# One reciprocal and one product with the gates per head, in place of one of each per query block

## The chip, the cores and the metric

The kernel runs on one core of a Trainium2 chip, in one launch. The metric is the device time of an execution in microseconds, as a median over runs. A core has five engines that work side by side, each through its own instruction queue in order: PE (matrix products; PEld is its weight load), DVE (VectorE), ACT (ScalarE), POOL (GpSimd) and SP, which here only issues transfers.

## The reference, cut to what matters

A two-layer decoder trunk over 512 tokens of width 1024. Each layer is a gated feed-forward half-step, a mixer, and a second gated feed-forward half-step. The mixer merges a pooling branch with an attention branch of 16 heads of width 64, and each head adds three attentions, each weighted by a gate:

```
out = gc[..., 0:1] * o_cmp + gc[..., 1:2] * o_slc + gc[..., 2:3] * o_win
# o_slc, o_win: p = masked_softmax(s, mask);  o = p @ v
# masked_softmax: exp(s - max) / sum(exp(s - max))
```

With 512 tokens there are 8 blocks of 64 keys and 16 would be selected, so the selected branch sees all earlier keys, and so does the window of 512. The two branches therefore need the same kind of causal softmax, each over its own keys; `gates` holds the sigmoids of the gates, three for each head and token.

## The kernel before

All products run in float32 split in a high and a low part, three matmuls in place of one (`mm3`, lines 121 to 123). The weights are streamed from memory, and ACT and DVE split each piece (lines 114 and 115). The feed-forward steps are long rows of such projection matmuls, each with 512 columns.

In the mixer, `head_probs` and `head_out` handle one head each. `head_probs(h)` goes over four query blocks of 128 tokens. For each block and each of two branches (selected, window) PE makes the scores (lines 645 and 655), DVE adds the distance term and finds the row minimum (line 634, `softmax_num`), and ACT takes the exponential and its row sum (line 636). The row sums of a head lie in one tile `c` of 128 x 8, a column for each pair of block and branch. Then, for each query block, DVE inverts two columns of `c` (line 660), multiplies them with two gates (line 661), and scales the two blocks of exponentials by them (line 664). `head_out(h)` transposes the scaled blocks on PE (line 677) into three banks for each branch; the first bank takes key block 0 of all four query blocks. ACT and DVE split each bank into `ph` and `pl` (lines 114 and 115), and PE multiplies these with the values (line 691).

The program is written as a list of steps: `head_probs(h)`, then `head_out(h-1)`, then one or two units of projection work that fill the time (the lists `gp`, `ga` and `q`). The order in which instructions stand on each engine is not the written order: a scheduler orders them when the program is built, by which of them are ready, and it mixes the projection matmuls of the fill between the matmuls of the heads. PE and DVE both run 16 heads in each of two layers in this way; these two stretches are called head stages below.

Of the kernel before, what the change touches and what calls it, by code (L numbers as in the profile page):

```python
# [14 lines left out]
ALU = mybir.AluOpType  # L15
# [4 lines left out]
TB = T // P  # L20
# [31 lines left out]
class Trunk:  # L52
# [566 lines left out]
    def head_probs(self, h):  # L619

        nc = self.nc
        g, q = h // 8, self.qs.pop(h)
        m, c = self.sm(8, "m"), self.sm(8, "c")
        probs = self.probs[h] = {}

        def slot():
            i = self.tpos % 16
            self.tpos += 1  # L630
            return self.tbuf[i // 8][:, i % 8]

        def softmax_num(t, sp, i, nk):
            nc.vector.tensor_tensor_reduce(t, sp, self.dist[:, T - nk :], SLOPES[h], 3e38,  # L634
                                           ALU.add, ALU.min, m[:, i : i + 1])
            nc.scalar.activation(t, t, AF.Exp, scale=-1.0, bias=m[:, i : i + 1],  # L636
                                 accum_out=c[:, i : i + 1])

        for qb in range(TB):
            nk = P * (qb + 1)  # L640
            qq = q[:, qb * P : qb * P + P]
            if qb < 2:
                sp = self.bank("sc")[:, : 2 * nk]
                for i, K in enumerate((self.KH[g], self.KL[g])):
                    nc.tensor.matmul(sp, qq, K[:, :, :nk], start=i == 0, stop=i == 1)  # L645
                t2 = slot()[:, : 2 * nk].rearrange("p (r k) -> p r k", r=2)
                s2 = sp.rearrange("p (r k) -> p r k", r=2)
                for br in range(2):
                    softmax_num(t2[:, br], s2[:, br], 2 * qb + br, nk)
                    probs[qb, br] = t2[:, br]  # L650
            else:
                for br in range(2):
                    sp = self.bank("sc")[:, :nk]
                    for i, K in enumerate((self.KH[g], self.KL[g])):
                        nc.tensor.matmul(sp, qq, K[:, br, :nk], start=i == 0, stop=i == 1)  # L655
                    t = slot()[:, :nk]
                    softmax_num(t, sp, 2 * qb + br, nk)
                    probs[qb, br] = t
            ci = c[:, 2 * qb : 2 * qb + 2]
            nc.vector.reciprocal(ci, ci)  # L660
            nc.vector.tensor_mul(ci, ci, self.gates[:, qb, 3 * h + 1 : 3 * h + 3])
            for br in range(2):
                t = probs[qb, br]
                nc.vector.tensor_scalar(t, t, ci[:, br : br + 1], None, ALU.mult)

    def head_out(self, h):
        nc = self.nc
# [247 lines left out]
```

## Time and profile before

| | |
|---|---|
| median of 3 runs | 2397.09 us (2396.93 to 2399.38) |
| the profiled execution | 2397.52 us, span in the trace 2395.7 us |
| PE busy in the span | 2363.0 us, 99% |
| DVE busy in the span | 1398.9 us, 58% |
| ACT busy in the span | 977.4 us, 41% |
| head stage of the first layer | 497.2 to 757.4 us |
| head stage of the second layer | 1676.0 to 1936.3 us |

Busy shares are means over stages. The digits of DVE in 40 slices run from 3 and 4 in the feed-forward stages to 9 in the head stages, while PE shows 9 in all but the first and the last. The records of matmuls overlap, since they are pipelined. Records on DVE overlap a little too: an instruction's record runs on while the next has begun.

### The profile page before, as it was taken

The page shows a single profiled execution, that of the slowest core. Times are in us where ns is not written, and L with a number is a line of the kernel's source. Part 1 is how long each engine was busy: PE and PEld are TensorE (multiplying, and loading weights), DVE is VectorE, ACT ScalarE, POOL GpSimd, SP SyncE. Part 2 cuts the span into 40 slices and gives each one's busy share as a digit, 9 for nine tenths or more (in the row PEclk, how much of TensorE's full clock was granted, in tenths as well). Part 3 has the DMA queues.
Part 4 walks back from the last instruction along what each step waited for, and adds up shares of the span by engine and source line. Part 5 has one row for each costly group of instructions (what it writes and reads, how often), then busy time and mean ns, then how long its engine had stood idle before and what let it go on. Part 6 is the DMA issues. An engine that isn't in the chain of part 4 may idle for free.

```text
span 2395.7 us, 28552 instructions
## 1 busy us (share of the span) xinstructions
PE 2363.0 (99%) x11042; PEld 1955.6 (82%) x11042; DVE 1398.9 (58%) x2684; ACT 977.4 (41%) x1689; POOL 51.5 (2%) x106
## 2 busy tenths in 40 slices
PE   8999999999999999999999999999999999999998
PEld 6888888778888888888888888887888887888887
DVE  4434346768988544443544443567988975434444
ACT  4222235556666432222332222345666664322222
POOL 1000000000001000000000000000000010000000
PEclk9999999999999999999999999999999999999999
DMA  5323224522124432323223232334222253232321
GB/s 159 104 90 105 89 97 140 158 82 62 58 76 153 138 105 89 101 93 101 92 89 105 89 105 90 119 115 156 71 71 80 71 185 110 88 106 88 106 79 62
DMA packets 226007, 244.24 MB, mean 102 GB/s; under 512 B 8688, under 2 KB 206416, under 8 KB 225872
## 3 DMA queue, kind: packets, MB, share of 16 engines
q1 hardware_dynamic: 225696, 242.37, 31.6%
q8 instruction: 87, 1.43, 0.3%
q14 instruction: 48, 0.39, 0.1%
q10 hardware_dynamic: 176, 0.05, 0.0%
HBM read 223.53 MB, written 18.87 MB: 101 GB/s over the span
## 4 chain that ended last, share of the span: by engine, by line
PE 58%; issue 15%; DVE 1%; POOL 1%; ACT 0%; DMA 0%; POOLq 0%; DVEq 0%; ACTq 0%; SPq 0%
PE ps_mm L122 9%; PE ps_mm L121 9%; PE ps_mm L123 9%; PE ps_pv L691 4%; PE ps_sc L121 3%; PE ps_sc L123 3%; PE ps_sc L122 3%; PE ps_pt L121 3%; PE ps_pt L122 3%; PE ps_pt L123 3%; PE ps_pt L677 3%; PE ps_sc L655 2%; PE ps_sc L645 1%; PE ps_sc L584 0%; DMA bP<-dB 0%
## 5 line engine op out<-in xcount | busy, mean ns | idle before, releaser
L114 ACT ACTIVATE wh<-wr 128x1024 fp32r<-128x1024 f32 (+1 forms) x392 | 408.8, 1043 | 1082.5 <-PE ps_mm L122 399.8
L115 DVE TENSOR_TENSOR wl<-wr,wh 128x1024 fp32r<-128x1024 f32 (+1 forms) x392 | 470.1, 1200 | 78.8 <-ACT wh L114 77.3
L121 PE MATMUL ps_sc<-xh,wh 128*128 128x512 f32 x704 | 276.8, 393 | 2.2 <-ACT x L840 2.2
L123 PE MATMUL ps_sc<-xh,wl 128*128 128x512 f32 x704 | 274.7, 390 | 0.0
L122 PE MATMUL ps_sc<-xl,wh 128*128 128x512 f32 x704 | 274.4, 390 | 0.0
L122 PE MATMUL ps_mm<-act,wh 128*128 128x512 f32 x704 | 274.4, 390 | 0.0
L123 PE MATMUL ps_mm<-act,wl 128*128 128x512 f32 x704 | 273.9, 389 | 0.0
L121 PE MATMUL ps_pt<-xh,wh 128*128 128x512 f32 x704 | 273.9, 389 | 0.0
L122 PE MATMUL ps_pt<-xl,wh 128*128 128x512 f32 x704 | 273.9, 389 | 0.0
L123 PE MATMUL ps_pt<-xh,wl 128*128 128x512 f32 x704 | 273.9, 389 | 0.0
L121 PE MATMUL ps_mm<-act,wh 128*128 128x512 f32 x704 | 273.3, 389 | 0.0
L342 DVE SCALAR_TENSOR_TENSOR x<-ps_mm,x 128x512 f32<-128x512 f32 x96 | 66.4, 692 | 239.7 <-PE ps_mm L123 239.7
L333 DVE TENSOR_TENSOR u<-ps_pt,R 128x512 f32<-128x512 f32 x88 | 60.9, 692 | 245.6 <-PE ps_pt L123 245.6
L121 PE MATMUL ps_mm<-xh,wh 128*128 128x512 f32 x512 | 203.2, 397 | 0.0
L325 DVE TENSOR_TENSOR z<-ps_sc,R 128x512 f32<-128x512 f32 x88 | 60.9, 692 | 242.7 <-PE ps_sc L123 242.6
L123 PE MATMUL ps_mm<-xh,wl 128*128 128x512 f32 x512 | 200.8, 392 | 0.0
L122 PE MATMUL ps_mm<-xl,wh 128*128 128x512 f32 x512 | 200.6, 392 | 0.0
L121 PEld LDWEIGHTS ps_sc<-xh,wh 128*128 128x128 f32 x704 | 132.6, 188 | 30.9 <-ACT x L840 2.6
L636 ACT ACTIVATE tbuf<-tbuf,m 128x128 f32<-128x128 f32 (+3 forms) x256 | 142.2, 556 | 36.2 <-DVE m L634 28.3
L122 PEld LDWEIGHTS ps_sc<-xl,wh 128*128 128x128 f32 x704 | 132.6, 188 | 28.1 <-issue 1.0
L122 PEld LDWEIGHTS ps_mm<-act,wh 128*128 128x128 f32 x704 | 132.2, 188 | 28.5 <-DVE act L115 1.3
L123 PEld LDWEIGHTS ps_sc<-xh,wl 128*128 128x128 f32 x704 | 132.5, 188 | 27.9
(238 smaller groups left out, 3870.7 us busy)
## 6 DMA issues: line engine op xcount, KB each, us to landing
wr<-in_ffn_w_gate_dram SPq DMA_DIRECT2D x44, 1024.0 KB, 5.3
wr<-in_ffn_w_up_dram SPq DMA_DIRECT2D x44, 1024.0 KB, 5.3
wr<-in_w_in_dram SPq DMA_DIRECT2D x34, 1024.0 KB, 5.2
wr<-in_ffn_w_down_dram SPq DMA_DIRECT2D x32, 1024.0 KB, 4.9
wr<-in_ffn_w_down_dram SPq DMA_DIRECT2D x16, 768.0 KB, 4.2
wr<-in_w_branch_nsa_dram SPq DMA_DIRECT2D x8, 1024.0 KB, 5.3
wr<-in_w_out_dram SPq DMA_DIRECT2D x8, 1024.0 KB, 5.3
dx<-x SPq DMA_DIRECT2D x16, 256.0 KB, 2.8
```

The source lines that it names most:

```text
L114: self.nc.scalar.activation(hi, src, AF.Copy)
L115: self.nc.vector.tensor_sub(lo, src, f32(hi))
L121: self.nc.tensor.matmul(out, lh, rh, start=first and i == 0, stop=False)
L122: self.nc.tensor.matmul(out, lh, rl, start=False, stop=False)
L123: self.nc.tensor.matmul(out, ll, rh, start=False, stop=last and i == n - 1)
L325: nc.vector.tensor_mul(z, g, self.R)
L333: nc.vector.tensor_mul(u, up, self.R)
L342: nc.vector.scalar_tensor_tensor(x, o, 0.5, x, ALU.mult, ALU.add)
L636: nc.scalar.activation(t, t, AF.Exp, scale=-1.0, bias=m[:, i : i + 1], accum_out=c[:, i : i + 1])
L655: nc.tensor.matmul(sp, qq, K[:, br, :nk], start=i == 0, stop=i == 1)
L677: nc.tensor.transpose(tp[:, w : w + P], probs[qb, br][:, kb * P : kb * P + P], self.ident)
L691: nc.tensor.matmul(out[:, T - n :], lhsT, rhs, start=i == 0, stop=i == len(ops) - 1)
```

## The change

The reciprocal and the product with the gates move out of the loop over the query blocks. They now run once for a head, over all eight columns of `c`, when all eight row sums are there; after that a second loop scales all eight blocks. All line numbers from 664 on grow by one: the reciprocal stands on line 659, the product on 661, the scaling on 665, the transposes on 678, the products with the values on 692.

```
-            ci = c[:, 2 * qb : 2 * qb + 2]
-            nc.vector.reciprocal(ci, ci)
-            nc.vector.tensor_mul(ci, ci, self.gates[:, qb, 3 * h + 1 : 3 * h + 3])
+        nc.vector.reciprocal(c, c)
+        c3 = c.rearrange("p (b r) -> p b r", r=2)
+        nc.vector.tensor_mul(c3, c3, self.gates[:, :, 3 * h + 1 : 3 * h + 3])
+        for qb in range(TB):
             for br in range(2):
-                t = probs[qb, br]
-                nc.vector.tensor_scalar(t, t, ci[:, br : br + 1], None, ALU.mult)
+                t, i = probs[qb, br], 2 * qb + br
+                nc.vector.tensor_scalar(t, t, c[:, i : i + 1], None, ALU.mult)
```

The scheduler orders the head stages anew. On PE the matmuls before the first head stage, between the two, and nearly all after the second stand in the same order as before.

**First place: DVE, at the end of the first head of a layer.** The rows run from the score pass (line 634, here over 512 keys) of the last query block to the scaling of that block; `qn` and `q` are a query projection, `pc` the compressed branch, `wl` a split of weights. Before:

```order
L634 ISA tbuf,m<-ps_sc,dist 128x512
L634 ISA m 128x1
L661 TENSOR_TENSOR c<-c,gates 128x2
L568 SCALAR_TENSOR_TENSOR qn<-ps_mm,small,R 128x512
L664 TENSOR_SCALAR tbuf<-tbuf,c 128x384 x2
L660 RECIPROCAL c<-c 128x2
L634 ISA tbuf,m<-ps_sc,dist 128x128
L634 ISA m 128x1
L661 TENSOR_TENSOR c<-c,gates 128x2
L573 TENSOR_TENSOR q<-qn,q 64x512
L664 TENSOR_SCALAR tbuf<-tbuf,c 128x512 x2
```

The same place after the change:

```order
L115 TENSOR_TENSOR wl<-wr,wh 128x1024
L616 TENSOR_TENSOR pc<-ps_pt,pc 64x512
L659 RECIPROCAL c<-c 128x8
L568 SCALAR_TENSOR_TENSOR qn<-ps_mm,small,R 128x512
L661 TENSOR_TENSOR c<-c,gates 128x8
L634 ISA tbuf,m<-ps_sc,dist 128x128
L634 ISA m 128x1
L665 TENSOR_SCALAR tbuf<-tbuf,c 128x128 x2
L665 TENSOR_SCALAR tbuf<-tbuf,c 128x256 x2
L665 TENSOR_SCALAR tbuf<-tbuf,c 128x384 x2
L665 TENSOR_SCALAR tbuf<-tbuf,c 128x512 x2
L573 TENSOR_TENSOR q<-qn,q 64x512 x2
```

The eight scalings of a head now stand in one run behind the one product with the gates; the split `wl` has come ahead of them, one `q` has gone behind them.

**Second place: PE, the first head's transposes.** `ps_mm_3813` (before) and `ps_mm_3801` (after) are the same projection of the fill, whose matmuls with `xh_2371`, `xl_2372` are its seventh to ninth; `ps_pt_3738` and `ps_pt_3726` are the bank of key block 0, whose fourth transpose reads the last query block. Before:

```order
L121 MATMUL ps_mm_3813<-xh_2371,wh_3649 128x512
L122 MATMUL ps_mm_3813<-xl_2372,wh_3649 128x512
L123 MATMUL ps_mm_3813<-xh_2371,wl_3650 128x512
L677 MATMUL ps_pt_3738<-ident_64,tbuf_3518 128x128
L677 MATMUL ps_pt_3747<-ident_64,tbuf_3518 128x128
L677 MATMUL ps_pt_3755<-ident_64,tbuf_3518 128x128 x2
```

After:

```order
L121 MATMUL ps_mm_3801<-xh_2371,wh_3643 128x512
L122 MATMUL ps_mm_3801<-xl_2372,wh_3643 128x512
L678 MATMUL ps_pt_3726<-ident_64,tbuf_3518 128x128
L678 MATMUL ps_pt_3735<-ident_64,tbuf_3518 128x128
L678 MATMUL ps_pt_3743<-ident_64,tbuf_3518 128x128
L123 MATMUL ps_mm_3801<-xh_2371,wl_3644 128x512
L678 MATMUL ps_pt_3726<-ident_64,tbuf_3518 128x128
L678 MATMUL ps_pt_3735<-ident_64,tbuf_3518 128x128
L678 MATMUL ps_pt_3743<-ident_64,tbuf_3518 128x128 x2
```

The transposes of the earlier query blocks stand later, between the projection matmuls; the fourth one still follows the ninth matmul of this projection.

**Third place: PE, the transposes of the fourteenth head.** `ps_pt_6082` (before) and `ps_pt_5992` (after) are its bank of key block 0, and `ps_pv_5975` and `ps_pv_5891` gather the head before it. Before:

```order
L691 MATMUL ps_pv_5975<-ph_5955,V_2733 128x512
L691 MATMUL ps_pv_5975<-pl_5956,V_2733 128x512
L691 MATMUL ps_pv_5975<-ph_5963,V_2733 128x384
L677 MATMUL ps_pt_6082<-ident_64,tbuf_3519 128x128 x2
L677 MATMUL ps_pt_6082<-ident_64,tbuf_3518 128x128 x2
```

After:

```order
L692 MATMUL ps_pv_5891<-pc_5640,Vc_3441 128x512
L655 MATMUL ps_sc_5972<-KH_2647,q_5298 128x512
L655 MATMUL ps_sc_5972<-KL_2649,q_5298 128x512
L655 MATMUL ps_sc_5977<-KH_2647,q_5298 128x512
L655 MATMUL ps_sc_5977<-KL_2649,q_5298 128x512
L678 MATMUL ps_pt_5992<-ident_64,tbuf_3519 128x128 x2
L678 MATMUL ps_pt_5992<-ident_64,tbuf_3518 128x128 x2
```

The bank now follows the last product of the head before it, and the last two score pairs (`ps_sc_5972`, `ps_sc_5977`) of the head after it.

## Rows read from the trace of the kernel before

**Rows 1.** The page: span, busy time, share and instructions of two engines.
```profile
span 2395.7 us, 28552 instructions
...
PE 2363.0 (99%) x11042; PEld 1955.6 (82%) x11042; DVE 1398.9 (58%) x2684; ACT 977.4 (41%) x1689; POOL 51.5 (2%) x106
```

**Rows 2.** Stretches: length, PE, PEld, DVE, ACT, POOL busy, granted clock, DMA share, GB/s.
```profile
480.00:490.00 10.00, 8.06 (x26) 6.78 (x26) 3.29 (x10) 3.63 (x9) 0.00 (x0) 0.60 0.14 51
490.00:500.00 10.00, 10.00 (x44) 8.08 (x43) 1.89 (x3) 2.14 (x3) 0.00 (x0) 0.89 0.19 64
497.20:757.40 260.20, 258.53 (x1389) 214.51 (x1387) 235.24 (x727) 176.17 (x438) 6.45 (x7) 1.00 0.25 79
1676.00:1936.30 260.30, 258.48 (x1389) 214.42 (x1387) 235.37 (x727) 176.14 (x438) 5.50 (x5) 1.00 0.25 80
```

**Rows 3.** Single lines on DVE: count, shortest, median, longest in ns.
```profile
L660 DVE RECIPROCAL c<-c x128: 145/160/168, 505.8 to 1921.8; 128x2 f32<-128x2 f32 x128
...
L661 DVE TENSOR_TENSOR c<-c,gates x128: 140/156/524, 506.4 to 1922.4; 128x2 f32<-128x2 f32 x128
...
L664 DVE TENSOR_SCALAR tbuf<-tbuf,c x256: 269/380/488, 507.4 to 1923.3; 128x128 f32<-128x128 f32 x32, 128x256 f32<-128x256 f32 x32, 128x384 f32<-128x384 f32 x32, 128x512 f32<-128x512 f32 x32
...
L604 DVE RECIPROCAL cc<-cc x8: 246/248/252, 505.0 to 1878.5; 128x16 f32<-128x16 f32 x8
...
L606 DVE TENSOR_TENSOR cc<-cc,gates x8: 173/176/178, 505.4 to 1878.9; 128x16 f32<-128x16 f32 x8
```

**Rows 4.** Waits of PE's matmuls: us in total, times, longest.
```profile
PE ps_pt L610 <- POOL ec L607: 2.0, 8, 0.3
```

**Rows 5.** Timeline of DVE in the first head: start, us, engine, line.
```profile
507.41 0.47 DVE L664 TENSOR_SCALAR tbuf<-tbuf,c 128x128 f32<-128x128 f32 x2
507.80 0.15 DVE L660 RECIPROCAL c<-c 128x2 f32<-128x2 f32 x1
507.88 0.53 DVE L634 CUSTOM_DVE_ANT_0 tbuf<-ps_sc,dist 128x384 f32<-128x384 f32 x1
...
510.69 0.61 DVE L664 TENSOR_SCALAR tbuf<-tbuf,c 128x256 f32<-128x256 f32 x2
...
512.03 0.15 DVE L661 TENSOR_TENSOR c<-c,gates 128x2 f32<-128x2 f32 x1
512.11 0.75 DVE L568 SCALAR_TENSOR_TENSOR qn<-ps_mm,small,R 128x512 f32<-128x512 f32 x1
512.78 0.74 DVE L664 TENSOR_SCALAR tbuf<-tbuf,c 128x384 f32<-128x384 f32 x2
...
513.89 0.69 DVE L573 TENSOR_TENSOR q<-qn,q 64x512 fp32r<-64x512 f32 x1
514.61 0.88 DVE L664 TENSOR_SCALAR tbuf<-tbuf,c 128x512 f32<-128x512 f32 x2
```

**Rows 6.** Timeline of PE there: the group with the fourth transpose.
```profile
515.12 0.39 PE L123 MATMUL ps_mm<-xh,wl 128*128 128x512 f32 x1
515.35 0.60 PE L677 MATMUL ps_pt<-ident,tbuf 128*128 128x128 f32 x4
```

**Rows 7.** Timeline of DVE: the last scalings of the thirteenth and fourteenth head.
```profile
708.04 0.88 DVE L664 TENSOR_SCALAR tbuf<-tbuf,c 128x512 f32<-128x512 f32 x2
...
720.71 0.88 DVE L664 TENSOR_SCALAR tbuf<-tbuf,c 128x512 f32<-128x512 f32 x2
```

**Rows 8.** Timeline of PE: the transposes that follow those two.
```profile
711.21 0.60 PE L677 MATMUL ps_pt<-ident,tbuf 128*128 128x128 f32 x4
...
721.48 0.60 PE L677 MATMUL ps_pt<-ident,tbuf 128*128 128x128 f32 x4
```

**Rows 9.** The page's groups: split of weights, exponentials; busy us, mean ns of one.
```profile
L115 DVE TENSOR_TENSOR wl<-wr,wh 128x1024 fp32r<-128x1024 f32 (+1 forms) x392 | 470.1, 1200 | 78.8 <-ACT wh L114 77.3
...
L636 ACT ACTIVATE tbuf<-tbuf,m 128x128 f32<-128x128 f32 (+3 forms) x256 | 142.2, 556 | 36.2 <-DVE m L634 28.3
```

**Rows 10.** Timeline of PE: the wait ahead of the clock's fall.
```profile
482.09 0.39 PE L121 MATMUL ps_pv<-w2h,hh 128*128 128x64 f32 x1 [1.94 <-issue]
```

## The prediction

> **What bounds the kernel now.** I read the busy shares of the page first. PE is busy for 2363.0 of 2395.7 us, 99%; DVE, on which every changed instruction runs, for 1398.9 us, 58% [rows 1]. A mean over stages can hide a stage in which DVE sets the pace, so the second view is the busy time of the two head stages alone, the only places where lines 660 to 664 run [rows 2]. There DVE is busy for 235 of 260 us, 90%, but PE for 258.53 of 260.20 and 258.48 of 260.30, at the full granted clock (1.00). PE is thus idle for 1.67 and 1.82 us, 3.49 us together, and nothing done on DVE in these stages can win more than that by ending waits, as long as PE keeps its matmuls. It does: the scheduler deals out the same matmuls, in another order. The third view is what PE's matmuls waited for [rows 4]: 2.0 of the 3.49 us are the transposes of the compressed branch waiting for POOL, eight times, on which the change has no hold. About 1.5 us are left. The fourth is the timeline of both engines around the transposes of a head, to see how long a scaled block lies ready before PE takes it; there the price of a later scaling is decided.
>
> **What is removed and added.** Sixteen heads by two layers by four query blocks make 128 reciprocals of 128x2 at 160 ns and 128 products at 156 ns [rows 3]: 128 x 316 ns = 40.4 us of records. What comes is 32 of each at 128x8, a shape the trace does not hold. From below it is bounded by the 128x2 rows, 316 ns a pair, from above by the 128x16 rows, 248 + 176 = 424 ns [rows 3]: 10.1 to 13.6 us. I take the lower, whose 8 against 2 elements are the nearer pair, so 30.3 us of records go. What DVE's queue gains is less, since the records overlap: a reciprocal starts at 507.80 and the next instruction at 507.88, a product at 512.03 and the next at 512.11 [rows 5], 0.08 us each. The 192 instructions fewer free 192 x 0.08 = 15.4 us of DVE, 0.5 us a head. On the path this is worth 0 us: PE hides it, being the busy engine in both stages [rows 2]. Had DVE been the bound, this term would be a gain (a rival below). For the part of PE's idle time that is not POOL's I take half, **-0.7 us**, with 0 and -3.5 us as its ends.
>
> **What moves.** The scalings of query blocks 0 to 2 come after the last exponential of the head, as one run with those of block 3. For PE that matters at the bank of key block 0, whose fourth transpose reads block 3: ahead of that scaling now stand six others. They are two of 128 columns (507.41 to 507.80, 0.39 us), two of 256 (0.61 less the overlap of 0.08, 0.53 us) and two of 384 (0.74 less 0.08, 0.66 us) [rows 5], together 1.58 us by which the block can be late.
>
> How much of that shows depends on how long the block lies ready. In most heads it lies long: in the thirteenth head of the first layer the scaling of 128x512 starts at 708.04 and ends some 0.49 us later (the longest of line 664 is 488 ns [rows 3]), and PE takes it in the group at 711.21 [rows 7, 8], so 2.7 us are to spare. Measured in the same way, the 28 heads other than the first and the fourteenth of each layer have that much or more; this thirteenth head is the closest of them. A block late by 1.58 us is still early there: 0 us. Two heads a layer are close. In the first, the scaling starts at 514.61 and ends at about 515.10, and the transposes' group starts at 515.35, its weight load 0.2 us sooner [rows 5, 6]: nothing to spare. In the fourteenth it starts at 720.71, ends at 721.20, and is taken at 721.48 [rows 7, 8]: at most 0.3 us. If the order stood, these would cost 1.58 + 1.3 = 2.9 us a layer, 5.8 us in all, the upper end of this term.
>
> The order does not stand. In the first head (the first and second place of the section on the change) PE still does the same nine projection matmuls before the fourth transpose, so the block is wanted at the same time as before. DVE has this ahead of the scaling: more by the split `wl` of 1.20 us [rows 9], less by one `q`, 513.89 to 514.61, 0.72 us [rows 5], and less by three reciprocals and three products, 6 x 0.08 = 0.48 us. The sum is 1.20 - 0.72 - 0.48 = 0.0 us: the scaling should end about when it did. The new wait of the one reciprocal for the last exponential has `wl` and `pc` ahead of it on DVE, over 1.2 us of work against 0.56 us for a mean exponential [rows 9]; behind it in the queue stand `qn`, a score pass of the next head and the eight scalings. I put 0.2 us a layer on this head. In the fourteenth (third place) the transposes now follow the last two score pairs of the next head, while before they stood ahead of all of its passes over 384 and 512 keys: the cover grows by more than the 1.58 us, and the cost is 0. For splits `pl` that now queue behind the run of eight scalings I add 0.3 us for both layers, as a guess between 0 and 1.5 us. The term is **+0.7 us**, from 0 to +5.8.
>
> At this place a rule speaks against the change. The trace shows a DVE with 10% to spare in the stage and a PE that waits for 1.7 us there [rows 2]. The Trainium skill, page "Perfetto Trace Analysis", section "Optimizing Scalar/DVE Operations", says that grouping work into larger operations can raise throughput where the engine is saturated, but that where it is not, and it makes others wait, smaller pieces may let work end sooner. By its first half the sum would hold the 30.3 us as a gain, by its second it would be a loss, since PE gets its blocks later; the row stands nearer to the second, though with little to wait for.
>
> **The sum.** The profiled execution took 2397.52 us, 1.8 us more than its span. -0.7 + 0.7 = 0, so 2397.5 us against that execution; it lies 0.4 us over the median of the three runs, 2397.09, and against that median the forecast is **2397.1 us, no change**. A difference of under 0.2%, 4.8 us, counts as no change for this kernel. By the ends of both terms the forecast's own range is 2393.6 to 2402.9.
>
> **The rivals.**
> - *The late block shows (slower).* In the first and fourteenth head of each layer PE stands still until the run of scalings has reached block 3. For it: there is nothing to spare in the first head. Against it: the shorter DVE queue and the moved transposes, as worked out. It decides if DVE, delayed by `wl` or by the wait for the last exponential, ends the scaling over a microsecond after PE has come to it. Price 5.8 us: 2402.9. Chance 12%.
> - *The clock falls (slower).* In the first layer, ahead of the heads, PE stood idle for 1.94 us until 482.09 [rows 10], and the granted clock of the next stretches was 0.60 and 0.89, part of the time at its lower level of 1.2 GHz [rows 2]: 0.40 x 10 + 0.11 x 10 = 5.1 us lost. A new wait of that length in a head stage could do the same: 2397.1 + 1.9 + 5.1 = 2404.1. No wait in the head stages came near that length, and both ran at 1.00. Chance 3%.
> - *That fall stays away (faster).* It lies ahead of everything that moves, so only chance would take it out: 2397.1 - 5.1 = 2392.0. Chance 5%.
> - *DVE is the bound after all (faster).* Then 30.3 us would go: 2366.8. PE's 99% in these very stages speaks against it. Chance 2%.
> - That the change does not do what it says is left out: the order shows the one reciprocal and one product of 128x8 in each head.
>
> **How the numbers follow.** No change 78%, slower 12 + 3 = 15%, faster 5 + 2 = 7%. The range 2392.0 to 2403.0 holds the forecast with its own ends, the first rival and the third; outside lie the clock's fall and a bound on DVE, 5%, and what I have not thought of.
>
> **What would show it.** In the profile after, lines 659 and 661 should show 32 instructions each at 160 to 250 ns, DVE in the head stages should be busy for 10 to 15 us a stage less, and the stages should last 260 us with PE idle for 1 to 3 us. A wait of PE's transposes on line 678 for line 665, above all at about 515 us, would speak for the first rival; a clock under 1.00 inside a head stage for the second; a stage shortened by 5 us or more would prove the reading of the bound wrong.

## The result and the profile after

The changed kernel takes 2413.06 us (median of 4 runs, 2409.86 to 2417.82), the kernel before beside it 2397.43 us (4 runs). The ratio is 1.0070, with an interval of 1.0057 to 1.0082: 15.6 us slower, and outside the forecast range.

The page after, span and busy times, to be held against [rows 1]:

```profile
span 2408.0 us, 28410 instructions
...
PE 2367.2 (98%) x11042; PEld 1952.2 (81%) x11042; DVE 1385.9 (58%) x2492; ACT 969.3 (40%) x1689; POOL 49.6 (2%) x106
```

DVE has its 192 instructions fewer and 13.0 us less work, and PE the same 11042 matmuls; the span is 12.3 us longer. The two head stages after, from the first score matmul to the end of the last product with the values (columns as in [rows 2]; a granted clock of 1.00 is PE's full speed):

```profile
491.76:760.11 268.35, 263.16 (x1399) 215.63 (x1398) 229.25 (x631) 172.24 (x438) 6.45 (x7) 1.00 0.23 77
1681.85:1950.41 268.56, 263.23 (x1399) 215.60 (x1398) 229.26 (x631) 172.25 (x438) 5.50 (x5) 1.00 0.23 76
```

The same stretches of the kernel before, cut by the same two events (0.4 us longer than those of [rows 2]):

```profile
497.23:757.80 260.57, 258.90 (x1390) 214.87 (x1389) 235.64 (x727) 176.14 (x438) 6.45 (x7) 1.00 0.25 80
1675.99:1936.73 260.74, 258.92 (x1390) 214.81 (x1389) 235.80 (x727) 176.15 (x438) 5.50 (x5) 1.00 0.25 79
```

A stage is 7.8 us longer. Nine more matmuls of the fill fall in it, at a spacing of 0.227 us some 2.0 us that are missing elsewhere; 5.7 us a layer are lost. PE's idle time shows 5.2 - 1.7 = 3.5 us of that. The rest, about 2.2 us, stands in the busy column, since records overlap and a short wait leaves no gap between them.

The spacing of the matmuls' starts shows all of it. For each matmul of the stages I take the time since the start of the one before it, less the lower quartile of the same pair of shapes in the kernel before; the sum is the time lost by spacing. It grows by 11.6 us for both layers, 5.8 us a layer: by 5.3 us ahead of products with the values, by 3.2 us ahead of transposes of the scaled blocks, and by 3.1 us ahead of all others. The fifth and the ninth head take 1.4 us each of a layer's 5.8 us, the fourth and the eighth together 1.2 us.

What PE's matmuls wait for, after (us in total, times, longest):

```profile
PE ps_pv L692 <- ACT ph L114: 3.8, 8, 0.7
...
PE ps_pv L692 <- DVE o L696: 2.1, 6, 0.4
PE ps_pt L610 <- POOL ec L607: 1.8, 8, 0.3
PE ps_pt L678 <- DVE pl L115: 1.5, 4, 0.4
...
PE ps_pt L678 <- DVE pc L616: 0.9, 4, 0.2
```

The POOL row is that of [rows 4]. The other four are waits of `head_out`; of them the kernel before has only the one for `o`, with 0.8 us. No row names line 665, the scaling. The weight loads of these matmuls did wait for splits before the change too, but for less time. The kernel before, first layer:

```profile
PEld ps_pv L691 <- ACT ph L114: 3.7, 11, 0.8
...
PEld ps_pt L677 <- DVE pl L115: 1.2, 3, 0.4
```

The changed kernel, first layer:

```profile
PEld ps_pv L692 <- ACT ph L114: 6.7, 13, 0.9
...
PEld ps_pt L678 <- DVE pl L115: 1.8, 3, 0.8
```

PE waits for what ACT makes out of a transposed bank (`ph`), for banks that its next transposes are to fill and that DVE still reads (`pl`, `pc`), and for the bank of the products, which the head before has not left (`o`).

One place where that is seen is the fifth head of the first layer. PE, after:

```profile
570.48 0.39 PE L123 MATMUL ps_mm<-xh,wl 128*128 128x512 f32 x1
570.71 0.28 PE L645 MATMUL ps_sc<-KH,q 128*128 128x256 f32 x1
...
578.13 0.71 PE L678 MATMUL ps_pt<-ident,tbuf 128*128 128x128 f32 x5
578.62 0.39 PE L645 MATMUL ps_sc<-KH,q 128*128 128x256 f32 x1
578.85 0.28 PE L645 MATMUL ps_sc<-KL,q 128*128 128x256 f32 x1
579.35 0.55 PE L678 MATMUL ps_pt<-ident,tbuf 128*128 128x128 f32 x3 [0.22 <-DVE pc L616]
580.60 0.50 PE L692 MATMUL ps_pv<-ph,V 128*128 128x512 f32 x1 [0.71 <-ACT ph L114]
580.94 0.39 PE L121 MATMUL ps_mm<-xh,wh 128*128 128x512 f32 x1
```

ACT at the same time:

```profile
578.53 0.60 ACT L636 ACTIVATE tbuf<-tbuf,m 128x384 f32<-128x384 f32 x1
...
579.12 0.71 ACT L636 ACTIVATE tbuf<-tbuf,m 128x512 f32<-128x512 f32 x1
...
579.95 0.60 ACT L114 ACTIVATE ph<-ps_pt 128x512 fp32r<-128x512 f32 x1
```

The `ph` for which PE waits stands on ACT behind two exponentials of the next head. From 570.71 to 580.94, 10.2 us, PE has not one projection matmul (in the rows left out too), so nothing covers the wait. PE of the kernel before, at the same head:

```profile
577.97 0.45 PE L691 MATMUL ps_pv<-pc,Vc 128*128 128x512 f32 x1
578.26 0.39 PE L122 MATMUL ps_mm<-xl,wh 128*128 128x512 f32 x1
578.49 0.39 PE L123 MATMUL ps_mm<-xh,wl 128*128 128x512 f32 x1
...
580.09 1.25 PE L677 MATMUL ps_pt<-ident,tbuf 128*128 128x128 f32 x10
581.38 0.50 PE L691 MATMUL ps_pv<-ph,V 128*128 128x512 f32 x1
581.71 0.39 PE L121 MATMUL ps_mm<-xh,wh 128*128 128x512 f32 x1
```

Ten transposes stand there in a row, the product with `ph` follows without a wait, and projection matmuls stand on both sides. From the last product of the fourth head to that of the fifth, PE does 34 projection matmuls before and 23 after; the ninth head of each layer reads the same. That is no general rule: in other heads that lose, such as the seventh (24 after, 21 before, a wait of 0.33 us for `o`), the fill is not short.

### The profile page after: what moved, and what is told of

Same layout as the page of the kernel before. It is cut to its first block, busy times and chain, and to the rows that moved or that the text cites. A ratio compares the mean times of both kernels' runs of the same rounds, so it can differ in the third digit from the quotient of the medians.

```text
span 2408.0 us, 28410 instructions
## 1 busy us (share of the span) xinstructions
PE 2367.2 (98%) x11042; PEld 1952.2 (81%) x11042; DVE 1385.9 (58%) x2492; ACT 969.3 (40%) x1689; POOL 49.6 (2%) x106
## 4 chain that ended last, share of the span: by engine, by line
PE 46%; issue 16%; DVE 2%; DMA 1%; ACT 1%; POOL 1%; POOLq 0%; DVEq 0%; SPq 0%; ACTq 0%
PE ps_mm L122 7%; PE ps_mm L121 7%; PE ps_mm L123 7%; PE ps_sc L121 3%; PE ps_sc L123 3%; PE ps_sc L122 3%; PE ps_pt L122 3%; PE ps_pt L121 3%; PE ps_pt L123 3%; PE ps_pv L692 2%; PE ps_pt L678 1%; PE ps_sc L655 1%; DMA sA<-dA 1%; DVE wl L115 0%; POOL bP L781 0%
## 5 line engine op out<-in xcount | busy, mean ns | idle before, releaser
L123 PEld LDWEIGHTS ps_pt<-xh,wl 128*128 128x128 f32 x704 | 132.1, 188 | 27.5
```

The lines of the kernel that those rows point to most:

```text
L123: self.nc.tensor.matmul(out, ll, rh, start=False, stop=last and i == n - 1)
```

## The experiments

Each is timed beside the kernel before on the same chip, and the ratios are against it.

**The scalings late, the small operations as before.** Reciprocal and product stay with each query block; only the scalings go behind the last block:

```
+        for qb in range(TB):
             for br in range(2):
-                t = probs[qb, br]
-                nc.vector.tensor_scalar(t, t, ci[:, br : br + 1], None, ALU.mult)
+                t, i = probs[qb, br], 2 * qb + br
+                nc.vector.tensor_scalar(t, t, c[:, i : i + 1], None, ALU.mult)
```

> The kernel before with one part of the change alone: each query block keeps its own reciprocal and product of 128x2 in the loop, but the eight scalings of a head stand in a loop behind the fourth block. Theory A (late data: blocks that are scaled late, in one run, hold up PE) and theory B (order: with the scaling late, the scheduler spends the fill of projection matmuls early, and none is left beside the head's own work): both say that the late scaling does it, so 2406 to 2414 us, and from the first score matmul of a head stage to the product that spreads the next norm (line 273) about 6 us more than before (350.6 us in the first layer). Theory C (the merged reciprocal and product themselves, or the clock's fall ahead of the heads, cost the time): 2396 to 2400 us.

Measured: 2406.92 us, ratio 1.0039 (1.0019 to 1.0058), +9.7 us; a head stage lasts 265.1 us against 260.6, with the same DVE work (235.7 us against 235.6). So theory C falls: over half of the loss comes without any merged operation and without more work on DVE. Between A and B this run does not decide.

**The order of one kernel forced on the other.** PE's matmuls are bound to the other kernel's order by added dependencies in the build, which hold no semaphore:

```
+    for a, b in zip(rank, rank[1:]):
+        tc.add_manual_dep(pe[b], pe[a].name, ...)
```

The other engines are ordered anew around it. The changed instructions in the order of before:

> The changed kernel, all its instructions, with PE's 11,012 matmuls and transposes held to the order in which they stand in the kernel before; the other engines are scheduled around that. Theory A (late data): PE waits at the transposes, 2403 to 2413 us. Theory B (PE's order): with the old order the time goes back, 2396 to 2400 us. The prediction on record has 5.8 us as its upper end for this very case (if the order stood), so up to 2403 us.

The instructions of before in the order of after:

> The kernel before, with a reciprocal, a product and scalings for each query block, but PE held to the order in which it stands in the changed kernel. Theory A (late data): the data come early, PE finds them ready, 2395 to 2400 us. Theory B (PE's order): the order brings the loss with it, 2405 to 2414 us.

Measured: 2472.90 us, 1.0315 (1.0294 to 1.0337), and 2470.49 us, 1.0302 (1.0285 to 1.0319). What PE waits for in the first of them:

```profile
PE ps_pv L692 <- DVE pl L115: 16.6, 18, 2.1
PE ps_pv L692 <- ACT ph L114: 14.3, 12, 2.4
PE ps_pt L678 <- DVE pl L115: 10.2, 8, 1.7
PE ps_pt L678 <- DVE tbuf L665: 8.8, 2, 4.4
```

And in the second:

```profile
PE ps_sc L645 <- DVE m L634: 12.3, 6, 2.7
PE ps_pt L677 <- DVE c L661: 9.9, 8, 2.1
PE ps_pt L677 <- DVE pl L115: 7.0, 11, 1.0
```

Neither theory of these two runs holds. Either order, with data that it was not made for, costs 73 to 76 us, almost five times the loss of the change. A part of that is the clock, whose mean in the head stages was 0.98 in the first run and 0.99 in the second: an estimate by these shares is 0.02 x 596 = 12 us and 0.01 x 593 = 6 us. The first table also tests a sentence of the prediction, that with the order kept the two tight heads would cost 5.8 us: the scaling is waited for directly only in the first head of each layer (two waits, 4.4 us the longest), while 41 us are waits for splits. Why the earlier data of before do not simply fit the order of after stays open, since the pin reorders DVE and ACT as well. The second table does not decide it either.

**Two halves.** A reciprocal and a product of 128x4 behind each pair of blocks, and the four scalings of that pair:

```
+            if qb % 2:
+                ch = c[:, 2 * qb - 2 : 2 * qb + 2]
+                nc.vector.reciprocal(ch, ch)
...
+                for b in (qb - 1, qb):
```

> The changed kernel with two reciprocals and two products a head, each over two query blocks (128x4), and the scalings of these two blocks behind each: half as late, half as long a run of scalings. Theory A: about half the loss, 2400 to 2406 us. Theory B: the scheduler makes a third order, and the time goes by its luck, anywhere from 2396 to 2412 us. A loss of nothing would say that only the last step, waiting for all four blocks, costs.

Measured: 2396.68 us, 0.9994 (0.9981 to 1.0006); the head stages last 260.8 and 260.9 us. Theory A expected half the loss, so it misses; the time lies in the wide range of B. Of the 192 small operations that the change saves, 128 are saved here, DVE is relieved as much (229.6 us a stage against 229.3), and half of the lateness costs nothing.

**Late, without the run of scalings.** The kernel before, and at the end of a head six multiplications by 1.0 (made from the last sum) on a few columns of blocks 0 to 2. They hold these blocks until the last sum of the head is there, but occupy DVE for little:

```
+        one = self.sm(1, "one")
+        nc.vector.tensor_scalar(one, c[:, 7:8], 0.0, 1.0, ALU.mult, ALU.add)
+        for qb in range(TB - 1):
+            for br in range(2):
+                t = probs[qb, br][:, ::P]
+                nc.vector.tensor_scalar(t, t, one, None, ALU.mult)
```

In the expectations of this run and the next, D is the theory that the long run of scalings on DVE delays the splits, and E that the blocks are ready late.

> The kernel before, scalings early, with six short multiplications by 1.0 (128x1 to 128x3, one column of each 128) on the blocks of query blocks 0 to 2 once the last exponential of the head is there: the transposes get these blocks as late as in the changed kernel, but DVE has a run of about 0.6 us there in place of 2.1 us. Theory D (the run): the run of scalings on DVE holds up splits and row minima that PE and ACT wait for, so without it little is lost, 2396 to 2401 us. Theory E (lateness): the blocks come late, the scheduler arranges PE around that, and the time stays lost, 2404 to 2412 us.

Measured: 2407.25 us, 1.0050 (1.0034 to 1.0067), +11.3 us. Nothing of the reciprocals, products and scalings was touched, and most of the loss is there, as E expects; D expected at most 2401 us. It is not quite clean, since 224 small operations come on top (DVE 246 us a stage against 236); the first experiment, which adds no DVE work, loses 9.7 us too.

**The scalings on POOL.**

```
-                nc.vector.tensor_scalar(t, t, c[:, i : i + 1], None, ALU.mult)
+                nc.gpsimd.tensor_scalar(t, t, c[:, i : i + 1], None, ALU.mult)
```

> The changed kernel with its eight scalings a head on POOL, which is idle there, in place of DVE: no run on DVE at all, and 2.9 us of 16.3 us a head less to do for it, but the scaled blocks come later still (POOL took 1.05 us for 128x512 of another product). Theory D: the loss goes, 2392 to 2400 us, perhaps below the kernel before. Theory E: the loss grows, 2412 to 2440 us.

Measured: 2454.81 us, 1.0244 (1.0221 to 1.0268). DVE is relieved, to 194 and 195 us a stage, and the time goes up by 58.9 us:

```profile
PE ps_pt L678 <- POOL tbuf L665: 34.5, 24, 2.4
```

The two head stages (columns as in [rows 2]):

```profile
492.72:778.23 285.51, 266.69 (x1384) 217.43 (x1383) 194.06 (x503) 172.87 (x438) 147.99 (x135) 0.97 0.22 73
1702.08:1992.08 290.00, 270.12 (x1384) 219.92 (x1383) 195.41 (x503) 173.75 (x438) 145.84 (x133) 0.96 0.22 72
```

The stages are 54.2 us longer together than those of the kernel before. The direct waits for POOL are 34.5 us of that, and the granted clock, by its mean, takes some 20 us (an estimate, 0.03 x 285.5 + 0.04 x 290.0). So blocks that come this late cost, with DVE relieved; but these two terms fill the whole growth, and the run does not decide between D and E. Against D speaks the run before it.

**The load of the second compression weight, earlier.** In some executions the granted clock fell ahead of the heads [rows 2, 10], which blurs all comparisons. PE stands there for `w2r`, whose load of 64 KB is issued just before it is wanted. Both kernels were run with this load issued earlier, into a buffer of its own (the edit, shown in part, also moves the small tile `rcol` to another pool):

```
+            if i == 2 * which:
+                st["w2r"] = self.unit("w2r", 1, F32, "w2r", (P, 128)).rearrange(...)
+                nc.sync.dma_start(st["w2r"], w2.rearrange("(c p) d -> p c d", p=P))
...
-        nc.sync.dma_start(w2r, w2.rearrange("(c p) d -> p c d", p=P))
```

The kernel before with it:

> The kernel before with the small load w2r (64 KB) issued one or more steps earlier into a buffer of its own, ahead of the large weight load that it queued behind; PE's order is the same. If the wait of 1 to 2.4 us for that load brings on the clock's fall in some executions and layers, the falls go: 2387 to 2392 us, and a narrower spread than the 2392 to 2403 us seen over 14 runs. If the fall has another cause, 2394 to 2399 us.

The changed kernel with it:

> The changed kernel with the same earlier load. If the clock's falls and the loss in the head stages are two things that add up, the difference to the kernel before with the earlier load is 12 to 13 us, the loss of the head stages alone, so 2399 to 2405 us; if the falls were part of the loss, the difference shrinks to under 8 us.

Measured: 2391.18 us, 0.9983 (0.9973 to 0.9992), and 2405.34 us, 1.0039 (1.0026 to 1.0052). The difference is 14.2 us, about the whole loss. In both traces the clock ahead of the heads is 1.00, so its fall has no part in this difference; the head stages last 260.9 and 261.2 us in the first, 268.2 and 268.6 us in the second. In the first of the two the stretch of [rows 2] runs at the full clock:

```profile
480.00:490.00 10.00, 10.00 (x50) 7.79 (x49) 3.71 (x11) 4.66 (x11) 0.00 (x0) 1.00 0.33 121
```

**Both together: halves and early load.**

> Two reciprocals and two products of 128x4 per head, each behind a pair of query blocks, together with the early load of the second compression weight. If the two edits are independent, as both runs apart suggest (2396.68 against 2397.19 for the halves, 2391.18 against 2395.91 for the early load), this takes 2390 to 2392 us, faster than the kernel before by about 5 us. A rival, that the shorter DVE queue of the halves is worth something once the clock no longer hides it: below 2390 us. The other rival, that the halves cost a little which the spread of the kernel before had covered: 2393 to 2396 us.

Measured: 2388.76 us, 0.9969 (0.9957 to 0.9980), the fastest version, 7.2 us below the kernel before beside it (2395.91). Most of that is the early load's. The time lies in the range of the first rival, a gain of the halves: 2.4 us by the two medians. It is not shown, since the intervals of this run and of the early load alone (0.9973 to 0.9992) overlap.

**The step `head_out` of a head written ahead of the next head's scores**, in the changed kernel and, as a control, in the kernel before:

```
-            steps.append((None, lambda h=h: self.head_probs(h)))
             if h:
                 steps.append((None, lambda h=h: self.head_out(h - 1)))
+            steps.append((None, lambda h=h: self.head_probs(h)))
```

> The changed kernel, with head_out of head h-1 written ahead of head_probs of head h, so that the transposes and the splits ph and pl of a head come before the next head's exponentials wherever the scheduler has the choice. If what PE loses is that ph and pl stand behind the next head's exponentials and score passes on ACT and DVE, the waits of lines 678 and 692 should go and the time fall to 2397 to 2404 us. If the loss lies in the blocks being ready late, so that nothing is left on PE to put beside the splits, the order of writing does not help: 2409 to 2417 us. If the scores of the next head, now last in rank, come late in their turn, PE waits for row minima and exponentials instead: above 2417 us, and the next run is slower than the kernel before in the same way.

> The control for the run before it: the kernel before with the same exchange of the two steps. There PE waits for ph and pl for under 3 us in the head stages, so little can be won: 2393 to 2398 us by the first reading. If the next head's scores come late when they are last in rank: slower, above 2402 us. What the run before it takes is to be judged against this one: a difference of 13 us, as without the exchange, says that the exchange leaves the loss where it is; a difference under 6 us says that it removes it.

Measured: 2416.21 us, 1.0076 (1.0057 to 1.0095), and 2404.62 us, 1.0029 (1.0017 to 1.0041). The exchange does not cure the change: 11.6 us stay between the two. The kernel before loses 8.7 us by it, with no block late, so an order made anew can cost as much as that by itself. Whether `ph` behind exponentials makes the loss is not decided: with the exchange PE and its weight loads still wait for `ph`, 17.7 us in 56 waits against 17.2 us in 34 without it.

**Block 0 early, blocks 1 to 3 merged.**

```
+            if qb in (0, TB - 1):
+                b0 = 1 if qb else 0
+                ch = c[:, 2 * b0 : 2 * qb + 2]
+                nc.vector.reciprocal(ch, ch)
...
+                for b in range(b0, qb + 1):
```

> Block 0 of each head keeps a reciprocal, a product (128x2) and scalings of its own; blocks 1 to 3 share one reciprocal and one product of 128x6 behind the last exponential. The theory is that the loss comes from scaled blocks that are all ready late. If it counts how many blocks are late, three late ones lie between the halves (two pairs, no loss) and all four late (10 to 16 us): 2399 to 2407 us. If what counts is that PE can begin the transposes of a head with block 0 while the others are under way, one early block is enough: 2394 to 2399 us. If what counts is when blocks 1 and 2, with 256 and 384 keys, are ready, block 0 alone helps nothing: 2407 to 2416 us.

Measured: 2407.24 us, 1.0042 (1.0026 to 1.0058), +9.9 us. It lies at the edge of the first and third reading: by the medians one early block saves about a third of the loss, while merging in pairs saves all of it. Its interval reaches up to that of the change (1.0057 to 1.0082), so the third is uncertain. Blocks 1 to 3 have 2, 3 and 4 transposes a branch, block 0 only one.

## Why the prediction was wrong

*The bound and the removed work: right.* PE is the bound in the head stages; 13.0 us of DVE records went (30.3 less in small operations forecast, but the records overlap; 15.4 by the queue), and they bought nothing. The sign that the prediction names, 10 to 15 us less DVE work a stage, was too large: a stage shows 6.4 us less, since the 15.4 us are those of both. Lines 659 and 661 after (count, shortest, median, longest in ns) lie inside the bounds:

```profile
L659 DVE RECIPROCAL c<-c x32: 193/200/206, 506.9 to 1934.7; 128x8 f32<-128x8 f32 x32
...
L661 DVE TENSOR_TENSOR c<-c,gates x32: 156/162/174, 507.8 to 1935.4; 128x8 f32<-128x8 f32 x32
```

*The first head: close.* It was forecast at 0.2 us a layer; by the spacing of the starts it lost 0.6 us. DVE, after:

```profile
504.88 1.22 DVE L115 TENSOR_TENSOR wl<-wr,wh 128x1024 fp32r<-128x1024 f32 x1
506.13 0.69 DVE L616 TENSOR_TENSOR pc<-ps_pt,pc 64x512 fp32r<-64x512 f32 x1
506.86 0.20 DVE L659 RECIPROCAL c<-c 128x8 f32<-128x8 f32 x1
...
508.04 2.46 DVE L665 TENSOR_SCALAR tbuf<-tbuf,c 128x128 f32<-128x128 f32 x8
```

The scalings end at 510.50, 18.7 us into the stage against 17.9 us before, so 0.9 us later and not at the same time as forecast. PE's transposes go on there without a gap, the group of four at 510.16. In the whole trace PE's weight loads for transposes wait 1.3 us for a scaling, six times.

*The step that failed: what moves.* The prediction measured how long the **last** block lies ready and closed, for 28 heads: "A block late by 1.58 us is still early there: 0 us." That is the delay of block 3 alone, and a cover taken from the order of before. The other six scaled blocks are late by far more: in the first head of before, block 0 is scaled at 507.41 and block 3 at 514.61 [rows 5], 7.2 us apart, and after the change none is ready before the last sum. The scaled blocks still lie ready for PE in nearly all heads, as forecast. But the transposes of the early blocks can no longer begin early, and the scheduler lays the rest of the head out anew. The prediction put no cost on that; it saw the order move and took it, at the fourteenth head, as a relief.

The table has, as a mean over the 32 heads of a trace, the time from the start of a head's first score matmul to the start of its last product with the values, and the time lost by spacing in both head stages, as defined above, ahead of transposes of the scaled blocks and ahead of products with the values. The loss is against the kernel before beside each. The same kernels with the early load (before, two halves, changed) repeat the times by spacing within 0.4 us.

| kernel | blocks | a head, us | ahead of transposes, us | ahead of products, us | loss, us |
|---|---|---|---|---|---|
| before | early | 30.7 | 4.0 | 14.7 | |
| two halves | half late | 31.5 | 2.6 | 11.3 | 0 |
| before, steps exchanged | early | 26.8 | 3.8 | 19.3 | 8.7 |
| late scaling | late | 32.5 | 8.0 | 17.4 | 9.7 |
| block 0 early | three late | 32.8 | 7.7 | 17.4 | 9.9 |
| late without the run | late | 32.9 | 9.3 | 18.8 | 11.3 |
| changed | late | 35.3 | 7.2 | 20.0 | 15.6 |
| changed, steps exchanged | late | 27.0 | 8.9 | 16.3 | 20.3 |

All five kernels with late blocks lose 3 to 5 us more ahead of transposes than the kernel before, and none of the others does. That is the mark of the lateness. The larger part ahead of products is no such mark: the exchange of steps alone, with early blocks, brings it to 19.3 us, near the 20.0 us of the change. Nor does the length of a head set the loss, since with the exchange the heads are the shortest and both kernels are slower. How many scores of later heads fall between a head's last score and its last product does not set it either: 13.8 on average with two halves, which lose nothing, and 12.9 with late blocks and no run of scalings, which lose 11.3 us (12.6 before, 14.4 after the change).

*The term that was mis-sized with it* is "For splits `pl` that now queue behind the run of eight scalings I add 0.3 us for both layers, as a guess between 0 and 1.5 us." The loss in the head stages is 5.7 us a layer, 11.4 us for both, and the waits that PE's rows name for it are for `ph`, for banks that `pl` and `pc` still read, and for `o`. In the two profiled executions that is nearly the whole difference of 12.3 us; the medians lie 15.6 us apart, the profiled execution of the changed kernel being the fastest of its four (2409.86 us). A long run of scalings is not needed for it, as the run without one shows (11.3 us).

*The rivals.* "The late block shows" has the sign, but not the place: it put the price at the first and fourteenth head, where PE waits little (no more than 0.3 us at once); the largest single waits, 0.7 us, are in the fifth and ninth. No head stage left the full clock (1.00 in both rows above).

*The rule of the Trainium skill* ("Perfetto Trace Analysis", "Optimizing Scalar/DVE Operations") came out in its second half: where the engine is not saturated but makes others wait, smaller pieces may let work end sooner. This case agrees in the sign, with 1.0070 for four blocks merged and 0.9994 for two and two; DVE was busy for 235.6 of 260.6 us of a stage before.

*What stays open.* Shown is that blocks held back to the last sum of a head make the loss: added alone they cost 9.7 and 11.3 us, and taken back by half they cost nothing. Shown is also where it is paid, in the head stages, ahead of transposes and products. Not shown is why the scheduled order cannot absorb it, nor how much of each loss is the lateness and how much the chance of an order made anew, since such an order alone cost 8.7 us. Neither forcing an order nor exchanging two steps brought the loss back. By the medians the change loses some 6 us more than the late scaling alone, though the two intervals just touch; why is open too.

## What to carry to other kernels

A merged operation starts with its last input, so ask for every consumer of every piece, not only of the last one, how much later its input comes, and what then meets the work behind that point. Where a scheduler orders the program, a slack read from the order of before does not tell what the new order costs; a cheap test is to add the dependency alone, with tiny operations, and look at the time. Test a mere change of order beside it, as a control. Merging in halves kept two thirds of the saved instructions (128 of 192) at no cost.

## What the runs showed of the hardware

A small load can take as long as a large one. The 64 KB of `w2r` for the value branch took 6.9 us from issue to landing (median of the two layers, kernel before), while the loads of 1024 KB from `in_w_in_dram` took 5.2 us (median) and the 64 KB for the key branch 3.3 us:

```profile
w2r<-in_cmp_v_w_dram SPq DMA_DIRECT2D x2, 64.0 KB, 6.9
```

PE stood for 1.94 us [rows 10], and the granted clock was 0.60 in the 10 us that held the wait's end, part of the time at 1.2 GHz, its lower level. After the change the first layer's wait was 1.04 us and no fall followed (1.00 from 482 to 497 us), while in the second it was 2.44 us and one did:

```profile
1668.29 0.27 PE L121 MATMUL ps_pv<-w2h,hh 128*128 128x64 f32 x1 [2.44 <-issue]
```

```profile
1670.00:1680.00 10.00, 10.00 (x34) 8.19 (x33) 2.35 (x6) 3.21 (x6) 0.00 (x0) 0.67 0.16 59
```

With the load issued earlier no instruction waits for `w2r` any more, and the runs of the kernel before, 2391.06 to 2398.10 us in that comparison, draw together to 2390.08 to 2393.29.
